# A two-layer decoder trunk: two weight differences placed behind the low parts, and a shorter tail left behind one channel-major matmul

## The chip, the cores and the metric

The kernel runs on one core of one Trainium2 chip. The metric is device time in microseconds of one execution, the median of several runs; lower is better. TensorE (PE, with its weight loads PEld), VectorE (DVE), ScalarE (ACT), GpSimd (POOL) and SyncE (SP, which issues the weight loads from HBM) each work through their own list of instructions in order.

## The reference

256 positions, width 2048, two layers, float32. Cut to what matters:

```python
for l in range(DEPTH):                       # 2
    h = rms_norm(x, norm1_g[l])
    z = h @ w_in[l]                          # 2048 -> 5120
    q, k, v, gu, gv = jnp.split(z, splits, axis=-1)
    attn = dilated_attention(rotary(q), rotary(k), v)          # 8 heads of 128
    gm = chunked_gmlp(gelu(gu), gelu(gv), ...)                 # 8 groups of 128
    x = x + jnp.concatenate([attn, gm], -1) @ w_out[l]
    h2 = rms_norm(x, norm2_g[l])
    x = x + jnp.square(jax.nn.relu(h2 @ w_up[l])) @ w_down[l]  # 2048 -> 8192 -> 2048
return rms_norm(x, final_g)
```

## The kernel before

**Products in two parts.** Every float32 operand is split into a high part (`hi`, a float32r copy made by ScalarE) and a low part (`lo`, the rest, a subtraction on VectorE). A product is three matmuls: high by high, high by low, low by high. Weights come in blocks of 128x1024 (`raw`, 7 buffers), loaded by SP, split on ScalarE (L168, or L186 for half a block) and VectorE (L178, L191), and then used by TensorE. Activations lie in `hs` or `half`, split in the same way (L645 high, L648 low).

**Steps.** All matmul work is a list of steps, one or four weight blocks each, and the program text is written out in the order of that list. `ahead` blocks before a step is due, its high parts are written (`high_to`), then its low parts (`low_to`), then the step's matmuls. Three kinds of step matter. A *natural* step (L464 to L466) has activations as stationary operand. A *channel-major* step (`transposed`, L404) has 128x128 pieces of a weight block as stationary operand, 256 positions as moving one, 24 matmuls per block. A *seven-product* step (`fast`, L434) is used for part of the down matrices: on a 2x2 split of positions and output columns it forms seven products instead of eight, in the manner of Strassen and Winograd, with sums of weights and sums of activations (`shared`). It needs four weight blocks: `Top`, `Bottom` and two `Sums`. There are 76 such steps in the run, each between two channel-major ones; the table `ORDER` and `USUAL` say where.

**The sums of weights.** `Top` and `Bottom` are split for their left halves (`Top`) or whole (`Bottom`). Then `Sums.high` of the first sum forms in place, in the raw buffers, t.left = t.right - t.left (L219) and t.right = b.right - t.right (L220); ScalarE copies that block as the high part of the first sum; VectorE goes on with b.right = b.right - t.left (L223) and b.left = b.right - b.left (L224), from which the second sum's high part is copied. Each of these four runs on 128x512 elements. The low parts of the sums (L178) follow.

**Matmuls left behind.** A seven-product step issues 42 matmuls, of which the last `BEHIND` are not written at the step's end but kept in `left_over`. The next channel-major step writes them after its first `BETWEEN` matmuls. The first of that step's matmuls waits for its high part (from ScalarE), the second for its low part (from VectorE).

Of the kernel before, what the change touches and what calls it, by code (L numbers as in the profile page):

```python
# [32 lines left out]
OP = mybir.AluOpType  # L33
# [32 lines left out]
USUAL = ((7, 9), (2, 3), (13, 14))  # L66
WARM = 11
HALVES = 5
BEHIND, BETWEEN = 3, 2
D_SCORES, D_NORM, D_TURN, D_VALUES = 2, 1, 3, 2  # L70


# [19 lines left out]
def trunk(ctx: ExitStack, tc: tile.TileContext, layout, xT, consts, gains, w, b_sp, w_sp, out):  # L92
# [11 lines left out]
    vec, act, pe = nc.vector, nc.scalar, nc.tensor  # L104
# [40 lines left out]
    class Sub:  # L145
# [4 lines left out]
        def __init__(self, *spec):  # L150
            self.i = len(layout)
            self.kc, self.n = spec[-2:]
            layout.append(spec)
# [7 lines left out]
        def high(self, parts, between=None):  # L161
            self.h = wp.tile([P, 1024], F32R, name="hi", tag="hi", bufs=HI_BUFS)
            self.hi = self.h.rearrange("p (k n) -> p k n", n=self.n)
            m = 1024 // parts
            for j in range(parts):
                if between and j:
                    between()
                act.activation(self.h[:, j * m:(j + 1) * m], self.raw[:, j * m:(j + 1) * m], AF.Copy)  # L168

        def low(self, parts, between=None):  # L170
            lo = wp.tile([P, 1024], F32R, name="lo", tag="lo", bufs=LO_BUFS)
            self.lo = lo.rearrange("p (k n) -> p k n", n=self.n)
            m = 1024 // parts
            for j in range(parts):
                r = slice(j * m, (j + 1) * m)
                if between and j:
                    between()
                vec.tensor_tensor(lo[:, r], self.raw[:, r], self.h[:, r].bitcast(F32), op=OP.subtract)  # L178

    class Top(Sub):  # L180
# [7 lines left out]
        def low(self, parts):  # L188
            lo = wp.tile([P, 1024], F32R, name="lo", tag="lo", bufs=LO_BUFS)
            self.lo = lo[:, 0:512].rearrange("p (k n) -> p k n", k=2)  # L190
            vec.tensor_tensor(self.lo, self.left(), self.hi.bitcast(F32), op=OP.subtract)  # L191

        def left(self):
            return self.raw.rearrange("p (k n) -> p k n", k=2)[:, :, 0:256]
# [6 lines left out]
    class Bottom(Sub):  # L201


        left, right, frees = Top.left, Top.right, 0

    class Sums(Sub):


# [1 line left out]

        def __init__(self, top, bottom, second):
            self.top, self.bottom, self.second = top, bottom, second
            self.n = 512

        def high(self, parts):
            t, b = self.top, self.bottom
            self.raw = (b if self.second else t).raw
            if not self.second:
                vec.tensor_tensor(t.left(), t.right(), t.left(), op=OP.subtract)  # L219
                vec.tensor_tensor(t.right(), b.right(), t.right(), op=OP.subtract)  # L220
            Sub.high(self, 1)
            if not self.second:
                vec.tensor_tensor(b.right(), b.right(), t.left(), op=OP.subtract)  # L223
                vec.tensor_tensor(b.left(), b.right(), b.left(), op=OP.subtract)  # L224
# [287 lines left out]
    def layer(l, n1, n2, n3, last):  # L512
# [130 lines left out]
        def to_half(t, c, src, wait=False):  # L643

            act.activation(t[:, c:c + 2, 0, :], src, AF.Copy)  # L645

            def low():
                vec.tensor_tensor(t[:, c:c + 2, 1, :], src, t[:, c:c + 2, 0, :].bitcast(F32), op=OP.subtract)  # L648

            if wait:  # L650
                behind.append((now[0] + 1, low))
            else:
                low()
# [419 lines left out]
```

## Time and profile before

| what | value |
|---|---|
| median of 3 runs | 2032.55 us (2028.91 to 2033.97) |
| profiled execution | 2032.09 us, span 2030.3 us |
| granted TensorE clock | 0.998 |
| HBM | 394.58 MB read, 205 GB/s over the span |
| L404, matmuls of channel-major steps | 12480 |
| L434, matmuls of seven-product steps | 3192 |

In the rows that follow in the prediction, a timeline row is: start in us from the span's start, duration in us, engine, line, operation, output and inputs by the program's names, shape, and the count of instructions merged into the row; a bracket at its end is idle time of the engine before it and what ended it. A row of the waits is: engine, what it issued, what it waited for, then us in total, times, and the longest. Matmuls are pipelined, so a matmul's duration is longer than the time until the next one starts.

### The profile page before, as it was taken

The numbers are of one execution on the slowest core, as the hardware profiler recorded it, in microseconds if no ns is written. First come the engines' busy times: TensorE is split into PE (matmuls) and PEld (weight loads), VectorE is DVE, ScalarE is ACT, GpSimd is POOL, SyncE is SP. The second block draws the span as 40 slices with busy tenths as digits, with TensorE's granted clock in tenths as the row PEclk, the third lists the DMA queues.
The fourth block names the chain that finished last, engine by engine and source line by source line (L and its number), as shares of the span: only waits on it lengthen the run. The fifth ranks groups of instructions, "written<-read, shape, count | busy, mean of one in ns | idle before, by whom it ended". The sixth has DMA issues, their size and how long they took to land.

```text
span 2030.3 us, 40718 instructions
## 1 busy us (share of the span) xinstructions
PE 2016.9 (99%) x16834; PEld 1979.6 (98%) x16834; DVE 1576.8 (78%) x1950; ACT 1213.2 (60%) x1613; POOL 157.1 (8%) x200
## 2 busy tenths in 40 slices
PE   9999999999999999999999999999999999999997
PEld 7998999999999999999989989999999999999997
DVE  7566766688888898888856667667888898888985
ACT  7565454566566666665545654556666666667654
POOL 0002300000001000100000033000000000010000
PEclk9999999999999999999999999999999999999999
DMA  8554556567677776866664455555676776778562
GB/s 326 192 168 166 187 187 200 175 229 207 217 221 237 244 225 193 243 214 210 204 212 166 167 187 188 188 196 180 217 228 209 226 236 215 239 212 263 183 211 93
DMA packets 126443, 419.27 MB, mean 207 GB/s; under 512 B 14128, under 2 KB 22064, under 8 KB 126256
## 3 DMA queue, kind: packets, MB, share of 16 engines
q1 hardware_dynamic: 110800, 389.86, 56.6%
q0 software_dynamic: 14304, 23.86, 6.8%
q8 instruction: 132, 2.16, 0.4%
q10 hardware_dynamic: 1152, 2.94, 0.4%
q14 instruction: 55, 0.45, 0.1%
HBM read 394.58 MB, written 22.02 MB: 205 GB/s over the span
## 4 chain that ended last, share of the span: by engine, by line
PE 97%; DVE 2%; DMA 1%; ACT 0%; issue 0%; ACTq 0%; SPq 0%; DVEq 0%
PE acc L404 69%; PE acc L434 9%; PE aux L434 8%; PE acc L466 3%; PE acc L465 3%; PE acc L464 3%; DVE lo L178 1%; PE aux L698 0%; PE aux L592 0%; PE aux L634 0%; DMA raw<-in_w 0%; PE aux L621 0%; DVE x L1035 0%; DMA x<-in_xT 0%; PE aux L595 0%
## 5 line engine op out<-in xcount | busy, mean ns | idle before, releaser
L168 ACT ACTIVATE hi<-raw 128x1024 fp32r<-128x1024 f32 (+1 forms) x817 | 836.1, 1051 | 496.2 <-DVE raw L220 232.6
L178 DVE TENSOR_TENSOR lo<-raw,hi 128x1024 fp32r<-128x1024 f32 (+1 forms) x817 | 963.6, 1213 | 155.9 <-ACT hi L168 152.7
L404 PE MATMUL acc<-hs,hi 128*128 128x256 f32 x5632 | 988.1, 277 | 0.0
L404 PEld LDWEIGHTS acc<-hs,hi 128*128 128x128 f32 x5632 | 858.4, 188 | 0.3 <-issue 0.2
L404 PE MATMUL acc<-hs,lo 128*128 128x256 f32 x2816 | 779.0, 277 | 0.0
L404 PEld LDWEIGHTS acc<-hs,lo 128*128 128x128 f32 x2816 | 528.8, 188 | 0.5 <-issue 0.2
L404 PE MATMUL acc<-half,hi 128*128 128x256 f32 x2688 | 462.1, 276 | 0.0
L404 PEld LDWEIGHTS acc<-half,hi 128*128 128x128 f32 x2688 | 406.5, 188 | 0.0
L404 PE MATMUL acc<-half,lo 128*128 128x256 f32 x1344 | 371.1, 276 | 0.0
L404 PEld LDWEIGHTS acc<-half,lo 128*128 128x128 f32 x1344 | 252.4, 188 | 0.0
L871 POOL DMA_DIRECT2D far<-ar x92 | 74.7, 983 | 1158.9 <-ACT ar L874 607.0
L434 PE MATMUL acc<-hi,shared 128*128 128x256 f32 x768 | 139.1, 276 | 0.0
L434 PE MATMUL aux<-hi,half 128*128 128x256 f32 x528 | 120.6, 278 | 0.0
L434 PEld LDWEIGHTS acc<-hi,shared 128*128 128x128 f32 x768 | 119.3, 188 | 0.0
L434 PE MATMUL acc<-lo,shared 128*128 128x256 f32 x384 | 106.5, 277 | 0.6 <-DVE lo L178 0.6
L464 PE MATMUL acc<-hi,hs 128*128 128x512 f32 x256 | 101.3, 396 | 0.2 <-ACT hs L286 0.2
L466 PE MATMUL acc<-hi,hs 128*128 128x512 f32 x256 | 100.8, 394 | 0.0
L465 PE MATMUL acc<-lo,hs 128*128 128x512 f32 x256 | 100.1, 391 | 0.6 <-DVE lo L178 0.6
L648 DVE TENSOR_TENSOR half<-ar,half 128x512 fp32r<-128x512 f32 x72 | 49.7, 690 | 62.3 <-ACT half L645 61.2
L434 PEld LDWEIGHTS aux<-hi,half 128*128 128x128 f32 x528 | 92.9, 188 | 0.0
L434 PE MATMUL aux<-hi,shared 128*128 128x256 f32 x448 | 81.1, 276 | 0.0
L504 DVE TENSOR_TENSOR x<-x,acc 128x512 f32<-128x512 f32 (+1 forms) x49 | 33.0, 674 | 57.7 <-PE acc L404 57.3
(151 smaller groups left out, 1954.0 us busy)
## 6 DMA issues: line engine op xcount, KB each, us to landing
raw<-in_w SPq DMA_DIRECT2D x731, 512.0 KB, 4.6
far<-ar POOLq DMA_DIRECT2D x60, 256.0 KB, 6.3
far<-ar POOLq DMA_DIRECT2D x32, 128.0 KB, 4.4
ar<-far POOLq DMA_DIRECT2D x12, 256.0 KB, 8.9
raw<-in_w SPq DMA_DIRECT2D x10, 256.0 KB, 5.1
x<-in_xT SPq DMA_DIRECT2D x7, 256.0 KB, 5.9
out<-x SPq DMA_DIRECT2D x7, 256.0 KB, 3.0
shared<-in_b_sp ACTq DMA_DIRECT2D x2, 512.0 KB, 8.1
```

The costliest lines, as they stand in the source:

```text
L168: act.activation(self.h[:, j * m:(j + 1) * m], self.raw[:, j * m:(j + 1) * m], AF.Copy)
L178: vec.tensor_tensor(lo[:, r], self.raw[:, r], self.h[:, r].bitcast(F32), op=OP.subtract)
L404: pe.matmul(o, lhsT=lhs, rhs=xs[:, rhs, :], start=(first and j == 0), stop=(last and j == 2), skip_group_check=True)
L434: calls.append(lambda k=k, j=j, lhs=lhs, rhs=rhs: pe.matmul(o[n], lhsT=lhs, rhs=rhs, start=(p == 0 and k == 0 and j == 0 and n in fresh), ...
L464: pe.matmul(ps, lhsT=xh, rhs=hi, start=(k0 + k == 0), stop=False)
L465: pe.matmul(ps, lhsT=xh, rhs=lo, start=False, stop=False)
L466: pe.matmul(ps, lhsT=xl, rhs=hi, start=False, stop=(k0 + k == KC - 1))
L504: vec.tensor_tensor(xj, xj, ps[j][:, 0:S] if alone else pair(ps)[:, j, :], op=OP.add)
L648: vec.tensor_tensor(t[:, c:c + 2, 1, :], src, t[:, c:c + 2, 0, :].bitcast(F32), op=OP.subtract)
L871: nc.gpsimd.dma_start(far[g][:, r], src, **({} if e == max(g, 1) else {"accum_op": OP.add}))
```

## The change

Two parts. First, the two subtractions that form t.left and t.right (L219 and L220 before) leave `Sums.high` and stand right behind the low part of `Top` and of `Bottom` (L192 and L210 after); for that the first `Sums` tells `Bottom` its `Top`. Second, `BEHIND, BETWEEN` go from 3, 2 to 2, 1. The order of ScalarE, GpSimd and SP is not changed.

```diff
--- before.py
+++ after.py
@@ -66,7 +66,7 @@
 USUAL = ((7, 9), (2, 3), (13, 14))
 WARM = 11
 HALVES = 5
-BEHIND, BETWEEN = 3, 2
+BEHIND, BETWEEN = 2, 1
 D_SCORES, D_NORM, D_TURN, D_VALUES = 2, 1, 3, 2
 
 
@@ -189,6 +189,7 @@
             lo = wp.tile([P, 1024], F32R, name="lo", tag="lo", bufs=LO_BUFS)
             self.lo = lo[:, 0:512].rearrange("p (k n) -> p k n", k=2)
             vec.tensor_tensor(self.lo, self.left(), self.hi.bitcast(F32), op=OP.subtract)
+            vec.tensor_tensor(self.left(), self.right(), self.left(), op=OP.subtract)
 
         def left(self):
             return self.raw.rearrange("p (k n) -> p k n", k=2)[:, :, 0:256]
@@ -203,6 +204,11 @@
 
         left, right, frees = Top.left, Top.right, 0
 
+        def low(self, parts):
+            Sub.low(self, 1)
+            t = self.top
+            vec.tensor_tensor(t.right(), self.right(), t.right(), op=OP.subtract)
+
     class Sums(Sub):
 
 
@@ -210,14 +216,12 @@
 
         def __init__(self, top, bottom, second):
             self.top, self.bottom, self.second = top, bottom, second
+            bottom.top = top
             self.n = 512
 
         def high(self, parts):
             t, b = self.top, self.bottom
             self.raw = (b if self.second else t).raw
-            if not self.second:
-                vec.tensor_tensor(t.left(), t.right(), t.left(), op=OP.subtract)
-                vec.tensor_tensor(t.right(), b.right(), t.right(), op=OP.subtract)
             Sub.high(self, 1)
             if not self.second:
                 vec.tensor_tensor(b.right(), b.right(), t.left(), op=OP.subtract)
```

VectorE at the first seven-product step: `lo` with 128x512 is the low part of the top block, the next `lo` that of the bottom block, `raw<-raw` are the four subtractions. Before:

```order
L178 TENSOR_TENSOR lo<-raw,hi 128x1024
L191 TENSOR_TENSOR lo<-raw,hi 128x512
L178 TENSOR_TENSOR lo<-raw,hi 128x1024
L219 TENSOR_TENSOR raw<-raw 128x2x256
L220 TENSOR_TENSOR raw<-raw 128x2x256
L223 TENSOR_TENSOR raw<-raw 128x2x256
L224 TENSOR_TENSOR raw<-raw 128x2x256
```

After:

```order
L178 TENSOR_TENSOR lo<-raw,hi 128x1024
L191 TENSOR_TENSOR lo<-raw,hi 128x512
L192 TENSOR_TENSOR raw<-raw 128x2x256
L178 TENSOR_TENSOR lo<-raw,hi 128x1024
L210 TENSOR_TENSOR raw<-raw 128x2x256
L227 TENSOR_TENSOR raw<-raw 128x2x256
L228 TENSOR_TENSOR raw<-raw 128x2x256
```

One subtraction has moved ahead of the bottom block's low part; the second stands where it stood. At 10 of the 76 steps other work of VectorE lies between the two blocks' low parts, and the first subtraction moves ahead of that too. The first such place, after the change (L652 is L648 of before):

```order
L191 TENSOR_TENSOR lo<-raw,hi 128x512
L192 TENSOR_TENSOR raw<-raw 128x2x256
L652 TENSOR_TENSOR shared<-ar,shared 128x2x256 x2
L178 TENSOR_TENSOR lo<-raw,hi 128x1024
L210 TENSOR_TENSOR raw<-raw 128x2x256
```

TensorE at the end of the second seven-product step. `acc<-hs,...` is the channel-major step, `aux<-...,half` the seventh product. Before:

```order
L434 MATMUL aux<-lo,half 128x256
L434 MATMUL aux<-hi,half 128x256
L404 MATMUL acc_4577<-hs,hi 128x256
L404 MATMUL acc_4577<-hs,lo 128x256
L434 MATMUL aux<-hi,half 128x256
L434 MATMUL aux<-lo,half 128x256
L434 MATMUL aux<-hi,half 128x256
L404 MATMUL acc_4577<-hs,hi 128x256 x2
L404 MATMUL acc_4577<-hs,lo 128x256
```

After:

```order
L438 MATMUL aux<-lo,half 128x256
L438 MATMUL aux<-hi,half 128x256 x2
L408 MATMUL acc_4577<-hs,hi 128x256
L438 MATMUL aux<-lo,half 128x256
L438 MATMUL aux<-hi,half 128x256
L408 MATMUL acc_4577<-hs,lo 128x256
L408 MATMUL acc_4577<-hs,hi 128x256 x2
L408 MATMUL acc_4577<-hs,lo 128x256
```

The channel-major matmul on `lo`, which waits for VectorE, stands three matmuls later; the one on `hi`, which waits for ScalarE, one later.

## The prediction

> **What bounds the kernel now.** I read the page's busy shares first, then the first line of the chain that ended last, then the busy time by stretch, and last what TensorE waits for.
>
> ```profile
> span 2030.3 us, 40718 instructions
> PE 2016.9 (99%) x16834; PEld 1979.6 (98%) x16834; DVE 1576.8 (78%) x1950; ACT 1213.2 (60%) x1613; POOL 157.1 (8%) x200
> ...
> PE 97%; DVE 2%; DMA 1%; ACT 0%; issue 0%; ACTq 0%; SPq 0%; DVEq 0%
> ```
>
> TensorE is busy for 2016.9 of 2030.3 us and carries 97% of the chain. VectorE is at 78% on average, so an edit on VectorE counts only where VectorE is late for TensorE. These two stretches, an ordinary one and one in the up and down matrices near a layer's end, show that there are such places:
>
> ```profile
> 420.00:500.00 80.00, 80.00 (x706) 80.00 (x706) 66.77 (x76) 50.40 (x64) 6.51 (x9) 1.00 0.71 223
> 800.00:811.00 11.00, 10.80 (x94) 10.60 (x93) 10.82 (x12) 5.58 (x7) 0.00 (x0) 1.00 0.61 197
> ```
>
> After the stretch's length the columns are PE, PEld, DVE, ACT and POOL busy, the granted clock, the DMA share and GB/s. In 420 to 500 VectorE has 13 us of 80 free and PE none; in 800 to 811 VectorE is full (10.82 of 11.00) and PE loses 0.20. The clock is 1.00 in both. The lists of what PE and PEld waited for put all of the seven-product line's waits in two rows:
>
> ```profile
> PE acc L434 <- DVE lo L178: 0.6, 3, 0.2
> PEld acc L434 <- DVE lo L178: 1.3, 4, 0.4
> ```
>
> Four waits in the whole run, all for a low part. So the pool from which this change can draw is small, and the rest is the cost of the matmuls' order itself.
>
> **Edit 1, matmuls left behind (3 to 2, after one matmul instead of two).** No matmul is added or taken away; 76 seven-product steps are each followed by a changed row of eight or so. One such place before, on TensorE, with the next 256-column matmuls behind it:
>
> ```profile
> 495.25 0.28 PE L434 MATMUL aux<-hi,half 128*128 128x256 f32 x1
> 495.36 0.28 PE L404 MATMUL acc<-hs,hi 128*128 128x256 f32 x1
> 495.48 0.28 PE L404 MATMUL acc<-hs,lo 128*128 128x256 f32 x1
> 495.60 0.28 PE L434 MATMUL aux<-hi,half 128*128 128x256 f32 x1
> 495.72 0.28 PE L434 MATMUL aux<-lo,half 128*128 128x256 f32 x1
> 495.83 0.28 PE L434 MATMUL aux<-hi,half 128*128 128x256 f32 x1
> 495.95 0.40 PE L404 MATMUL acc<-hs,hi 128*128 128x256 f32 x2
> 496.19 0.28 PE L404 MATMUL acc<-hs,lo 128*128 128x256 f32 x1
> 496.30 0.39 PE L404 MATMUL acc<-hs,hi 128*128 128x256 f32 x2
> ...
> 497.32 0.28 PE L404 MATMUL acc<-hs,hi 128*128 128x256 f32 x1
> ```
>
> Durations overlap, so what a matmul costs is start to start. In the plain row from 496.30 to 497.32 nine matmuls take 1.02 us, 113.3 ns each. In the mixed row from 495.36 to 496.30 eight take 0.94, 117.5 ns each. The mixing costs 0.94 - 8 x 0.1133 = 0.033 us here, and with 76 places 2.5 us in the run. That is all that the order of matmuls costs today. The changed row has the same three switches between the two kinds (434 to 404, back, and to 404 again), but its mixed part is three matmuls long (one and two) and not five (two and three); with the three behind it that still read slow, six instead of eight. I take 6/8 of the cost: -0.6 us. Bounds: all of it goes (-2.5), or it doubles because a lone 404 matmul between two runs of 434 is worse (+2.5, another 0.033 at each of 76). The value lies near the middle, since the nearest row is the same pattern two matmuls longer.
>
> One place shows what the order of waits is worth. Near the end of layer 0 the low part for the next channel-major step was late:
>
> ```profile
> 925.54 0.19 PEld L404 LDWEIGHTS acc<-hs,hi 128*128 128x128 f32 x1
> 925.65 0.28 PE L404 MATMUL acc<-hs,hi 128*128 128x256 f32 x1
> 925.86 0.19 PEld L404 LDWEIGHTS acc<-hs,lo 128*128 128x128 f32 x1
> 925.86 0.39 PE L404 MATMUL acc<-hs,lo 128*128 128x256 f32 x1
> 925.96 0.19 PEld L434 LDWEIGHTS aux<-hi,half 128*128 128x128 f32 x1
> 926.08 0.28 PE L434 MATMUL aux<-hi,half 128*128 128x256 f32 x1
> ```
>
> The matmul on lo starts 0.21 after its forerunner instead of 0.11, and the three left-behind matmuls, which need nothing new, stand behind it: the first starts 0.22 later, because its weights were not loaded while the array waited. Loss: 0.10 + 0.11 = 0.21 us. In the changed order the matmul on lo stands three matmuls (0.34 us) further back, and the one on hi one matmul (0.11 us) further, so both get more time and nothing is asked for sooner; this loss goes: -0.2 us. It is a single place. What stands behind the waiting matmul is then the rest of the channel-major step, which needs the same low part anyway.
>
> The Trainium skill (TensorE: Matmul & The Clock Gate, "Step-by-step: what each phase is for") says that the queue pulls weight loads ahead of running matmuls while matmuls keep their order. By that rule the left-behind weights would be loaded during the wait and this place would give back 0.1 us, not 0.2. The rows at 925.86 and 925.96 speak against it here: the load behind the waiting one did not go ahead.
>
> **Edit 2, two subtractions moved.** 152 of VectorE's instructions move (76 of L219, 76 of L220), none is added. A row at the full stretch:
>
> ```profile
> 802.07 0.68 DVE L191 TENSOR_TENSOR lo<-raw,hi 128x512 fp32r<-128x512 f32 x1
> 802.67 1.22 DVE L178 TENSOR_TENSOR lo<-raw,hi 128x1024 fp32r<-128x1024 f32 x1
> 803.81 0.68 DVE L219 TENSOR_TENSOR raw<-raw 128x512 f32<-128x512 f32 x1
> 804.52 0.69 DVE L220 TENSOR_TENSOR raw<-raw 128x512 f32<-128x512 f32 x1
> 805.25 0.69 DVE L223 TENSOR_TENSOR raw<-raw 128x512 f32<-128x512 f32 x1
> 805.97 0.69 DVE L224 TENSOR_TENSOR raw<-raw 128x512 f32<-128x512 f32 x1
> 806.58 1.22 DVE L178 TENSOR_TENSOR lo<-raw,hi 128x1024 fp32r<-128x1024 f32 x1
> ```
>
> Start to start, a 512-wide one followed by one that does not touch its data takes 0.60 or 0.61 (L191, L224); one followed by an instruction that must wait for it takes 0.71 to 0.73 (L219, L220, L223). The difference, 0.11 us, is the price of two dependent instructions side by side. Before, three such pairs stand here: L219-L220, L220-L223, L223-L224. After, they are the top's lo with the first subtraction (it overwrites what lo has just read), the second subtraction with the third, and the third with the fourth; the second no longer follows the first directly. So three again: 0.72 + 0.60 + 1.14 + 0.72 + 0.72 + 0.61 = 4.51, against 806.58 - 802.07 = 4.51. On VectorE: 0. If I have one pair wrong, it is 0.11 us either way per site.
>
> What moves in time: the bottom's lo ends some 0.7 us later, and the subtraction that ScalarE waits for, with all behind it, ends when it did. ScalarE's wait there is its largest:
>
> ```profile
> ACT hi L168 <- DVE raw L220: 232.6, 76, 5.2
> ```
>
> 3.1 us each time, at every site, and yet PE waits four times only: this wait has cover. It shrinks only where VectorE had stood idle for the bottom's hi. In the full stretch nobody gains, and the late part is the sums' lo, last of the row:
>
> ```profile
> 806.81 0.28 PE L434 MATMUL acc<-lo,shared 128*128 128x256 f32 x1
> ...
> 807.26 0.39 PE L434 MATMUL acc<-hi,shared 128*128 128x256 f32 x2
> 807.85 0.38 PE L434 MATMUL acc<-lo,shared 128*128 128x256 f32 x1 [0.20 <-DVE lo L178]
> ```
>
> At 807.26 two matmuls take 0.59 instead of 0.23: 0.36 lost, and with an unhidden load behind it 0.47; four such waits make at most 1.9 us. They keep their time, since the sum in front of them does: 0, with bounds of -1.9 (all vanish) and +0.5 (0.11 later at each of four). The bottom's lo, now at 804.6 instead of 803.9, is needed at product 2; the row at 806.81 is the second matmul on a low part of product 3, six matmuls before it is 806.1: 1.5 us of cover left. Where that cover was used up, the next thing late would be this lo.
>
> At 10 of 76 sites low parts of the activations' sums stand between the two weights' low parts, and the subtraction goes ahead of them:
>
> ```profile
> 791.40 1.29 DVE L648 TENSOR_TENSOR shared<-ar,shared 128x512 fp32r<-128x512 f32 x2
> ...
> 796.85 1.29 DVE L648 TENSOR_TENSOR shared<-ar,shared 128x512 fp32r<-128x512 f32 x2 [0.25 <-ACT shared L645]
> ```
>
> The pair at 791.40 comes 0.7 us later; the pair at 796.85, which TensorE needs next, has the same work in front of it as before. Cost 0. ScalarE, POOL and SP issue the same in the same order; SP's loads wait for the last reader of raw, which is still the fourth subtraction or the sums' lo.
>
> **Sum.** Against the profiled execution's 2032.09 us (span 2030.3 and 1.8 around it): -0.6 - 0.2 + 0 = 2031.3. The median of the runs is 0.46 above that execution, so 2031.8 as a median.
>
> **Rivals.** (A) The forecast: small change of order, under 1 us. (B) All that can be won is won: the mixing cost 2.5, the late place 0.2 and the four waits 1.9: 2032.55 - 4.6 = 2028.0. For it: the pool exists in the rows. Against: three switches and three dependent pairs remain. Even this is -0.23%. (C) Slower: the lone channel-major matmul is too short a cover for the weights of the two behind it, and one load per site shows, 0.11 us as in the row at 926.08: 76 x 0.11 = 8.4, giving 2041.0. Against: at 495.60 the load behind the second 404 matmul was hidden with the same neighbours. It decides from 0.08 us per site on (6.1 us). By the rule of the Trainium skill above (TensorE: Matmul & The Clock Gate) it could not happen at all, since loads are pulled ahead. (D) The bottom's lo, 0.7 us later, comes too late in the full stretches: say six sites by up to 0.7 us, +4.2 us, 2036.8; against it stand the 1.5 us above. (E) The change doesn't do what it says: VectorE gets back no time because three dependent pairs stay. I hold this true, it is part of A.
>
> **How the numbers follow.** A 0.78, B 0.09, C 0.04, D 0.06, and 0.03 for something not seen (of either sign). 0.3% is 6.1 us, about what a measurement of this kernel can tell from no change; A, B and D lie inside it, C outside. Faster by more 0.03, within 0.91, slower 0.06. The range takes in B and D with half a microsecond beyond each: 2027.5 to 2037.3; the runs shown, 2028.9 to 2034.0, scatter inside it. For A alone it is 2030 to 2034 (bounds of -2.5 and +2.5 on the mixing).
>
> **What the changed profile would show.** PE busy again 99% with the same 16834 matmuls; in the mixed row six start-to-start times of about 117 ns and then 113; at the place near 926 the matmul on lo without its 0.21; VectorE's row per site 4.5 us long with the first subtraction at 0.72 behind the top's lo and the second followed by the third at 0.72; four waits of the seven-product line for lo, as long as now. The prediction is wrong if matmuls behind the lone 404 show 0.2 us start to start at most sites, or if PE's waits for low parts pass some 8 us.

## The result, and the profile after

| | median, us | lowest to highest | runs |
|---|---|---|---|
| before | 2031.82 | 2028.77 to 2033.97 | 21 |
| after | 2034.22 | 2031.79 to 2034.91 | 21 |

The ratio after to before is 1.0012, with a 95% interval of 1.0007 to 1.0018: slower by 0.12%, or 2.4 us, where -0.7 had been forecast. That lies within the 0.3% and within the range, but the sign is wrong and the interval leaves no change out, so there is something to find.

The page of after, its first lines:

```profile
span 2030.1 us, 40718 instructions
PE 2017.2 (99%) x16834; PEld 1980.4 (98%) x16834; DVE 1576.7 (78%) x1950; ACT 1214.1 (60%) x1613; POOL 157.7 (8%) x200
```

And what the seven-product line (L438 now) waited for:

```profile
PEld acc L438 <- DVE lo L178: 1.7, 4, 0.5
PE acc L438 <- DVE lo L178: 0.9, 4, 0.3
```

The matmuls are the same and so is the number of waits; by these rows the four are 0.3 to 0.4 us longer in all than before (0.9 and 1.7 for 0.6 and 1.3), which is far from 2.4. The profiled execution of after took 2031.91 us and is one of its fastest; the profiled one of before took 2032.09. Their spans differ by 0.2 us, so subtracting page from page tells nothing. The loss must be looked for in parts whose size differs from one execution to the next.

It shows in the chain that ended last. A row there is start in us, duration in us, engine, output, line, and how many instructions in unbroken sequence. These rows of before are the same piece of a channel-major step, 94 matmuls between two mixed rows:

```profile
480.43 10.67 PE acc L404 x94
506.35 10.67 PE acc L404 x94
811.06 11.07 PE acc L404 x94
897.77 10.67 PE acc L404 x94
1816.61 10.67 PE acc L404 x94
1901.25 11.07 PE acc L404 x94
```

And of after, where the piece has 95 matmuls because only one matmul stands ahead of the two left behind:

```profile
479.99 10.78 PE acc L408 x95
505.87 10.78 PE acc L408 x95
810.11 10.78 PE acc L408 x95
894.68 11.19 PE acc L408 x95
1814.01 11.20 PE acc L408 x95
1900.78 11.20 PE acc L408 x95
```

10.67 / 94 and 10.78 / 95 are both 113.5 ns for a matmul; 11.07 / 94 and 11.19 / 95 are both 117.8. No row here lies between. TensorE has two rhythms, steady paces, for the same instructions, 4.3 ns apart. No wait stands inside these pieces, and a row of the busy times over a slow piece of before shows the clock granted in full (the columns are those of the prediction's windows):

```profile
811.00:822.00 11.00, 11.00 (x96) 11.00 (x95) 8.85 (x11) 7.78 (x12) 3.51 (x4) 1.00 0.98 269
1816.00:1830.00 14.00, 14.00 (x126) 14.00 (x125) 11.59 (x13) 10.78 (x16) 3.46 (x4) 1.00 0.97 274
```

The second row is, but for its first 0.6 us, a piece in the fast rhythm. Both have a clock of 1.00 and DMA at 0.97 to 0.98, so neither of these makes the difference. The Trainium skill (TensorE: Matmul & The Clock Gate, "Back-to-back issue gap") has one spacing for an isolated matmul of width 256, 262 cycles at 2.4 GHz, by estimate 109 ns; the two rhythms here are both longer, and the measurement decides.

Summed over every matmul's start time, what stands above 113.3 ns in stretches of the slow rhythm is this, in us (0.2 of each sum is two short stretches near 340 and 1345, in every kernel):

| stretch | before | after |
|---|---|---|
| 807 to 876 | 2.55 | fast |
| 892 to 931 | 0.12, ends at 897.7 | 1.43 |
| 1811 to 1875 | 0.13, ends at 1816.6 | 2.41 |
| 1898 to 1937 | 1.43 | 1.47 |
| sum | 4.4 | 5.5 |
| span less the sum | 2025.9 | 2024.6 |

Each stretch begins at one of the four waits for a low part, near 807, 892, 1811 and 1898 us. A pair is the two seven-product steps that work on the same outputs; the waits stand in the second step of the pairs that the table `ORDER` puts at (1, 2), which are called late pairs below. One of the waits in after:

```profile
1810.27 0.39 PE L438 MATMUL acc<-hi,shared 128*128 128x256 f32 x2
1810.92 0.39 PE L438 MATMUL acc<-lo,shared 128*128 128x256 f32 x1 [0.26 <-DVE lo L178]
```

It ends at the next fp32 transposes of a finished group of outputs (L844 of before, L848 of after), or at the second of them. In before it also ended early twice, at the first mixed row behind the wait. After has no such end; one wait of its four, near 807, started nothing.

With that first stretch slow as well, at 2.4 us as in the kernel e1_tail_only below, the profiled 2031.91 would be 2034.3, near the median of 2034.22. The runs fall in two groups: 5 lie from 2031.79 to 2032.68 and 16 from 2034.02 to 2034.91, with nothing between and 2.2 us from middle to middle, about what the first or third stretch costs. Before has no such groups and scatters over 5.2 us. That the groups of after are this stretch on and off is an inference: only one execution of after has a profile.

### The profile page after: what moved, and what is told of

Its sections match the earlier page's. It is cut to its first block, busy times and chain, and to the rows that moved or that the text cites. A ratio compares the mean times of both kernels' runs of the same rounds, so it can differ in the third digit from the quotient of the medians.

```text
span 2030.1 us, 40718 instructions
## 1 busy us (share of the span) xinstructions
PE 2017.2 (99%) x16834; PEld 1980.4 (98%) x16834; DVE 1576.7 (78%) x1950; ACT 1214.1 (60%) x1613; POOL 157.7 (8%) x200
## 4 chain that ended last, share of the span: by engine, by line
PE 96%; DVE 3%; ACT 1%; issue 0%; DVEq 0%; ACTq 0%
PE acc L408 68%; PE acc L438 9%; PE aux L438 8%; PE acc L468 3%; PE acc L470 3%; PE acc L469 3%; DVE lo L178 1%; PE aux L702 0%; PE aux L596 0%; PE aux L638 0%; PE aux L625 0%; PE aux L995 0%; DVE shared L652 0%; DVE x L1039 0%; DVE lo L191 0%
## 5 line engine op out<-in xcount | busy, mean ns | idle before, releaser
L438 PE MATMUL acc<-hi,shared 128*128 128x256 f32 x768 | 139.0, 276 | 0.0
L438 PEld LDWEIGHTS acc<-hi,shared 128*128 128x128 f32 x768 | 119.4, 188 | 0.0
L438 PE MATMUL aux<-hi,half 128*128 128x256 f32 x528 | 111.1, 277 | 0.0
L438 PE MATMUL acc<-lo,shared 128*128 128x256 f32 x384 | 106.5, 277 | 0.9 <-DVE lo L178 0.9
L652 DVE TENSOR_TENSOR half<-ar,half 128x512 fp32r<-128x512 f32 x72 | 49.7, 691 | 62.5 <-ACT half L649 61.4
L438 PEld LDWEIGHTS aux<-hi,half 128*128 128x128 f32 x528 | 87.3, 188 | 0.0
L438 PE MATMUL aux<-hi,shared 128*128 128x256 f32 x448 | 81.3, 277 | 0.0
```

Source lines behind the costliest of these rows:

```text
L438: calls.append(lambda k=k, j=j, lhs=lhs, rhs=rhs: pe.matmul(o[n], lhsT=lhs, rhs=rhs, start=(p == 0 and k == 0 and j == 0 and n in fresh), ...
```

## The experiments

**Theory 1**: an operand that comes late to a seven-product step puts TensorE in the slow rhythm; the mixed row of three behind two sometimes ends it, the row of two behind one never does, so the shorter tail pays for each late operand until the transposes. The rivals: the loss lies in the subtractions on VectorE; the mixed rows or the waits themselves cost more; there is no loss beyond scatter.

### One part of the change alone

```diff
 e1_tail_only: before with
-BEHIND, BETWEEN = 3, 2
+BEHIND, BETWEEN = 2, 1
 e2_subs_only: after with
-BEHIND, BETWEEN = 2, 1
+BEHIND, BETWEEN = 3, 2
```

> The shorter tail alone (2 matmuls left behind, after 1), subtractions as before. Theory 1 (rhythm): after a late low part TensorE goes on at 117.7 ns per matmul instead of 113.3 until the fp32 transposes of a finished group; the row of 3 behind 2 can bring it back to 113.3, the row of 2 behind 1 cannot. Then this kernel has after's time, about 2034 us (+2.4 on before), most runs between 2034 and 2035 and none below 2031.5, and its profile shows slow stretches that reach from a late low part to the next transposes. Theory 2 (VectorE): the moved subtractions make low parts later. Then this kernel has before's time or up to 1.5 us less, 2030.3 to 2031.8.

> The two moved subtractions alone, tail as before (3 behind 2). Theory 1: before's time, 2031.8 within 1 us, with runs scattered over some 4 us from 2029 to 2034, because a slow stretch ends early in some runs and not in others. Theory 2: after's time plus the 1.5 us of mixing that the shorter tail saves, about 2035.5.

Against before on the same chip (2032.16), the tail alone took 2034.25 (2033.87 to 2034.77, 11 runs), 1.0011 [1.0002, 1.002]: nearly all of the 1.0012 that the whole change costs. The subtractions alone took 2033.0 (2030.98 to 2033.83, 11 runs), 1.0004 [0.9995, 1.0013], not to be told from before, with a wide scatter like before's. That interval would still hold a loss like that of the change; that the subtractions cost nothing rests on VectorE's rows further below. The chain of the tail alone has the slow rhythm at all four places:

```profile
479.55 10.78 PE acc L404 x95
809.76 11.20 PE acc L404 x95
896.55 11.19 PE acc L404 x95
1815.88 11.19 PE acc L404 x95
```

Its slow stretches sum to 7.8 us, its span less these is 2024.2. In the subtractions alone the mixed row behind the first wait ended the slow rhythm (0.13 us there), the other three places stayed slow: 5.9, and 2026.2 without. So the tail's rest is 1.7 us shorter than before's (2025.9 to 2024.2; 2026.2 to 2024.6 with the subtractions moved), and the stretches outweigh it. Not all of the 1.7 is the tail's. The chain's first piece of 48 channel-major matmuls starts at 52.31 in before, 52.21 in the subtractions alone, 52.10 in after and 51.67 in the tail alone, ahead of any mixed row: these executions begin up to 0.6 us apart. Less that, the rest is 1.1 to 1.5 us shorter.

### Moving the late operands

```diff
 e4_after_later (on after), e5_before_later (on before)
-ORDER = {1: ((7, 10), (13, 14)), 6: ((11, 14), (1, 2), (6, 7)), 7: ((6, 9), (1, 2)), 8: ()}
+ORDER = {1: ((7, 10), (13, 14)), 6: ((11, 14), (2, 3), (6, 7)), 7: ((6, 9), (2, 3)), 8: ()}
```

> After, with the seven-product steps that stand right behind the start of an up block for e = 6 and 7 placed one channel-major step later (1, 2 becomes 2, 3), so that VectorE has 2.7 us more of TensorE time for the same work. If the four waits for low parts go, theory 1 expects the slow stretches to go too: 5.3 us of slow rhythm in after's profile plus some 2 us of waits, so 2024 to 2027 us for all runs, with a scatter under 1.5 us. Theory 2 expects the waits alone to go, 2 us: 2032.

> Before, with the same later places. Theory 1: no waits and no slow stretches either, and the tail of 3 behind 2 costs the 1.5 us more of mixing that the profiles show in the ordinary stretches: 1.0 to 2.0 us above the after kernel with later places, 2025.5 to 2028.5. Theory 2 expects 2029.8, 2 us below before, and the after kernel with later places above it.

After with the late pairs one place later took 2033.57 (2032.63 to 2033.99), 1.0006 [0.9997, 1.0015]; before with the same 2035.3 (2032.96 to 2037.06), 1.0014 [1.0005, 1.0023]. The late operands did not go, they moved: waits begin at 829.89, 909.65, 1835.69 and 1915.46 of the first, and slow stretches run from there, or from a smaller wait 6 us ahead, mostly to the transposes. Channel-major matmuls now wait for a low part too, twice in each kernel:

```profile
PE acc L408 <- DVE lo L178: 1.3, 2, 0.7
PE acc L404 <- DVE lo L178: 2.2, 2, 1.3
```

The first row is of after with later places, the second of before with them. Both levels missed what theory 1 expected, since its premise, no late operand, was not met. Only the order of the two, the shorter tail ahead by 1.7 us, is as expected, and 0.9 of that lies in these new waits. This pair is inconclusive.

Relieving VectorE instead, by giving to GpSimd the low parts of the activations that stand in front of the late places:

```diff
 e6_after_relief (on after), e7_before_relief (on before)
-        def to_half(t, c, src, wait=False):
+        def to_half(t, c, src, wait=False, eng=vec):
...
-                vec.tensor_tensor(t[:, c:c + 2, 1, :], src, t[:, c:c + 2, 0, :].bitcast(F32), op=OP.subtract)
+                eng.tensor_tensor(t[:, c:c + 2, 1, :], src, t[:, c:c + 2, 0, :].bitcast(F32), op=OP.subtract)
...
-                to_half(hid[e][0], c // P, z, True)
+                to_half(hid[e][0], c // P, z, True, nc.gpsimd if e in (5, 6) and c == 768 else vec)
...
-                to_half(sum_parts[0], k, inner[:, k:k + 2, :])
+                to_half(sum_parts[0], k, inner[:, k:k + 2, :], False, nc.gpsimd if e in (5, 6) and k < 4 else vec)
```

> After, with three low-part subtractions of activations per layer and tight place (e = 5 and 6: the last one of the hidden half, and those of the first two sums) on GpSimd instead of VectorE, some 1.9 us of VectorE's time ahead of the places where the low part of the weights' sum was 0.4 us late. Theory 1 (rhythm): if the low parts are in time, there are no slow stretches: 7.8 us of slow rhythm and 2 us of waits less than the run with the shorter tail alone, so 2024 to 2026.5 us, all runs within 1.5 us. Theory 2 (the time lies in the waits, and the slow stretches come from DMA traffic or chance): 2 us below after, 2032.

> Before, with the same relief of VectorE. Theory 1: no late low parts, no slow stretches, and the longer tail costs its 1.5 us of mixing more: 1.0 to 2.0 us above the after kernel with relief, 2025 to 2028 us. Then the shorter tail is the better one where nothing is late. Theory 2: 2029.8, 2 us below before and 2 us below after with relief.

After with relief took 2038.84 (2038.5 to 2039.05, 5 runs), 1.0036 [1.0022, 1.0049]; before with it 2034.57 (2034.0 to 2037.96, 11 runs), 1.0018 [1.001, 1.0027]. Both were a miss: loads for the seven-product line waited 12 times instead of 4 in the first and 10 times in the second, and slow stretches grew to 9.1 us in the first. The timelines of VectorE and GpSimd in the first show why (rows between are left out):

```profile
787.12 0.69 DVE L805 TENSOR_TENSOR ar<-ar 128x512 f32<-128x512 f32 x1 [1.49 <-POOL half L652]
...
790.63 1.66 DVE L192 TENSOR_TENSOR raw<-raw 128x512 f32<-128x512 f32 x1
...
792.81 1.72 DVE L178 TENSOR_TENSOR lo<-raw,hi 128x1024 fp32r<-128x1024 f32 x1
...
785.79 1.29 POOL L652 TENSOR_TENSOR half<-ar,half 128x512 fp32r<-128x512 f32 x1 [6.23 <-ACT half L649]
...
790.07 3.37 POOL L652 TENSOR_TENSOR shared<-ar,shared 128x512 fp32r<-128x512 f32 x2 [2.16 <-issue]
```

VectorE first stands idle for 1.49 us until GpSimd has written the low part of `half`, a subtraction that takes VectorE itself 0.69 in after. Then, while GpSimd's two subtractions ran, VectorE's 128x512 took 1.66 us instead of 0.69 and its 128x1024 1.72 instead of 1.22; GpSimd's pair took 3.37 against 1.29 for one alone. The two engines hold each other up. The Trainium skill (SBUF — State Buffer, "SBUF: two separate sides") says that a VectorE instruction with two SBUF inputs and a GpSimd one that reads SBUF lock each other out of a shared pair of ports; these rows agree. The two 128x512 of `shared` taken off VectorE here are worth 1.38 us, and it lost 1.47 again in these two rows (0.97 and 0.50).

### A late operand by itself

```diff
 e8_after_late_at_3 (on after), in Sub.low
-                vec.tensor_tensor(lo[:, r], self.raw[:, r], self.h[:, r].bitcast(F32), op=OP.subtract)
+                for _ in range(getattr(self, "times", 1)):
+                    vec.tensor_tensor(lo[:, r], self.raw[:, r], self.h[:, r].bitcast(F32), op=OP.subtract)
 in fast
+            if row0 == 2048 and col0 == 512 and p == 1:
+                upper.times = 3
```

One low part per layer, at an early step with time to spare, is written three times, so that it comes late.

> After, with one low part of a weights' sum written three times (same values) at the second seven-product step of e = 3 in both layers, so that it comes some 0.7 us too late there, at 558 and 1562 us. Theory 1: from there on 117.7 ns per matmul, through all mixed rows, until the first fp32 transposes 310 us later: 2.8 us per 600 matmuls, some 9 us per layer beyond the wait, 18 to 20 us in all if both waits start the slow rhythm, 9 if one does: 2043 to 2056. Theory 2: 1.4 us of waits, 2036.

One run of 2034.20, span 2032.3; expected were 2043 to 2056. The two waits came, 1.0 us each, and behind them the rhythm was fast:

```profile
564.11 10.78 PE acc L409 x95
811.16 10.78 PE acc L409 x95
895.72 11.20 PE acc L409 x95
```

So theory 1 in its strong form, that any late operand starts the slow rhythm, is refuted. At the four places it did so in 30 of 32 cases, over the eight profiled kernels that came to all four in the fast rhythm; the two exceptions are after and this kernel near 807. What sets a start apart from a wait of 1.0 us is open.

### The tail as a switch

```diff
 e3_no_tail (on after)
-                for call in calls[:-BEHIND]:
+                for call in calls:
                     call()
-                left_over.extend(calls[-BEHIND:])
```

> After with no matmuls left behind: a seven-product step ends, and the channel-major step follows with no mixed row. Theory 1 in its strong form: the clean change from activations to weights as stationary operand starts the slow rhythm too, and only a mixed row ends it; then most of the up and down matrices' 11000 matmuls take 4.4 ns more, 35 to 48 us in all: 2065 to 2082. Weak form (only late operands start it): the mixing cost goes, 1.0 to 1.5 us below after: 2032.5 to 2033.

One run of 2040.42, span 2038.7. The strong form there, in which a clean change starts the slow rhythm and only a mixed row ends it, expected 2065 to 2082, the weak one 2032.5 to 2033; both missed. The rhythm changes without any wait, from one step to the next:

```profile
396.90 4.76 PE aux L438 x42
401.66 8.48 PE acc L408 x72
410.14 4.95 PE aux L438 x42
415.09 8.17 PE acc L408 x72
```

4.76 / 42 is 113.3 ns, 8.48 / 72 is 117.8, 4.95 / 42 is 117.9, 8.17 / 72 is 113.5. A clean exit, from seven-product matmuls straight to channel-major ones, turns a fast rhythm slow and a slow one fast. (In the first kind the weights are the moving operand, in the second the stationary one.) By the matmuls' start times, 74 of the 76 exits do so, 38 from fast to slow and 36 from slow to fast; the two that kept the slow rhythm, at 814.6 and 1823.5, stand right behind a late operand. The slow stretches sum to 15.8 us. A mixed row makes that change twice, and so mostly keeps the rhythm it found. This gives the second form of theory 1, theory 3 in the expectations: the change toggles, the mixed row of two behind one toggles twice. (Theory 4 there is that the slow stretches belong to the place, whatever stands there.) The second form foretells two things: a clean exit right behind a late operand ends the slow rhythm; a clean exit at an early step starts one that lasts.

The first, in three kernels:

```diff
 e12_after_clean_late (on after), e14_before_clean_late (on before), e10_tail_only_clean_late (on e1_tail_only)
-                for call in calls[:-BEHIND]:
+                stay = 0 if p == 1 and col0 == 512 and row0 in (5120, 6144) else BEHIND
+                for call in calls[:len(calls) - stay]:
                     call()
-                left_over.extend(calls[-BEHIND:])
+                left_over.extend(calls[len(calls) - stay:])
 e11_after_clean_at_2 (on after): row0 == 1024 instead of row0 in (5120, 6144)
```

The four steps named have no tail; the other 72 keep theirs.

> After, with the same four clean exits. Theory 3: 2034.2 - 7.1 = 2027.1 in runs in which all four late operands leave the slow rhythm; where one leaves the fast one, the clean exit makes it slow and the run is 1.4 or 2.4 us longer, up to 2030. Theory 4: 2034.

> Before (3 left behind 2), with the same four clean exits. Theory 3: the mixing of the longer tail costs some 1.5 us more than in the kernel with the shorter tail and clean exits: 2027.5 to 2030, below before by 2 to 4. Theory 4: before's 2031.7.

> The shorter tail alone (subtractions as before), but with no tail at the four steps where the low part is late (second seven-product step of the late pair, e = 6 and 7, both layers). Theory 3 (toggle): TensorE has two rhythms, 113.3 and 117.7 ns; a late operand leaves it in the slow one nearly always, each change from a seven-product to a channel-major matmul toggles it, so a row with a tail has two toggles and keeps what it found, and a step without a tail has one. Then the clean exit behind the late operand ends the slow rhythm there: 7.6 us of slow stretches less 0.5 up to the exit, 2034.25 - 7.1 = 2027.1, between 2026 and 2028.5 in all runs. Theory 4 (the slow stretches belong to the place: DMA traffic or a full VectorE): 2034 as without the edit.

Against before on the same chip (2031.15, 27 runs), after with clean exits took 2029.25 (2027.0 to 2030.75, 11 runs), 0.9986 [0.9977, 0.9994]: faster than both kernels. Its profiled execution, the fastest of the 11, has the slow rhythm end at the clean exit at all four places; here a piece has 96, since no matmul stands ahead of a tail:

```profile
809.91 10.89 PE acc L408 x96
894.47 10.90 PE acc L408 x96
```

Its slow stretches sum to 0.6 us, and the span of 2025.2 less these is 2024.6, the same as for after: nothing else has changed by as much. Before with the same exits took 2030.64 (2028.9 to 2032.78), 0.9998 [0.9989, 1.0006]; all four exits ended the rhythm, and its profiled span is 2027.1 with 1.1 slow, 2026.0 without. Of these 1.1, 0.4 lie in two short stretches further on, near 923 and 1927, each behind a channel-major matmul on `lo` that came 0.1 us late, as at 925.86 of before; after has neither. The tail alone with them took 2031.32 (2027.31 to 2032.92), 0.9998 [0.9989, 1.0007]; in its profile three of four exits ended the rhythm and the one near 892 did not:

```profile
810.14 10.90 PE acc L404 x96
894.72 11.31 PE acc L404 x96
```

So the exit ends it in 11 of 12 profiled cases, not always. The medians won less than that suggests: for the tail alone with clean exits 2026 to 2028.5 had been expected in all runs, and 2 of 11 lie there; for before with them 2027.5 to 2030, and 4 of 11 lie there. The profiled executions are among the fastest of their kernels, and in the slower ones more exits may have failed, which no profile shows.

The second:

> After, with one clean exit per layer at an ordinary step in time: the second seven-product step of the late pair of e = 2, at 475 and 1480 us. Theory 3: the exit toggles the fast rhythm to slow, and the mixed rows keep it so up to the late pair of e = 6, some 2930 matmuls by 4.35 ns = 12.7 us per layer, 25 in all: 2055 to 2061. Theory 4, and a reading in which the switch costs only its own few matmuls: 2034.

One run of 2058.56, span 2056.8, in the range expected of theory 3. Two exits, no late operand near them, and the slow rhythm stands from 480 to 881 and from 1498 to 1900, over 56 mixed rows that all keep it:

```profile
480.02 11.31 PE acc L408 x96
507.01 11.20 PE acc L408 x95
```

Without its slow stretches (34.2 us) the span would be 2022.6, 2 us less than for after. About 1 us of that is the mixed rows, counted in that sum though the fast rhythm pays 0.018 us for each as well; another 1.1 is two of the four waits, near 807 and 1811 in after, which did not occur here.

## Why the prediction was right or wrong

**The mixing cost: right sign, too small.** The mixed row of after, on TensorE, in the fast rhythm:

```profile
495.13 0.28 PE L408 MATMUL acc<-hs,hi 128*128 128x256 f32 x1
495.25 0.28 PE L438 MATMUL aux<-lo,half 128*128 128x256 f32 x1
495.37 0.28 PE L438 MATMUL aux<-hi,half 128*128 128x256 f32 x1
495.48 0.28 PE L408 MATMUL acc<-hs,lo 128*128 128x256 f32 x1
495.60 0.39 PE L408 MATMUL acc<-hs,hi 128*128 128x256 f32 x2
495.83 0.28 PE L408 MATMUL acc<-hs,lo 128*128 128x256 f32 x1
495.94 0.39 PE L408 MATMUL acc<-hs,hi 128*128 128x256 f32 x2
```

Six matmuls take 0.70 here, 116.7 ns each. In the chain, from one such piece to the next, lie the same matmuls and two sites: 480.43 to 506.35 is 25.92 us before, 479.99 to 505.87 is 25.88 after. That is 0.02 a site and 1.5 us for 76, where 0.6 had been forecast. By the start times of 47 such rows in each, a mixed row stands 0.039 us above the plain pace before and 0.018 after: half of the cost is left, not six eighths. The spans less slow stretches agree: 1.1 to 1.5 lower with the shorter tail when the different beginnings are taken off, the late place below included. In the slow rhythm the saving is not there: behind the first late place, where before and the tail alone are both slow, the changed row is some 0.015 longer. Rival C, an unhidden load at each site, has no such row.

**The late place near 926: right, 0.2.** In after the matmul on lo follows its forerunner at the pace around it:

```profile
924.08 0.28 PE L438 MATMUL aux<-hi,half 128*128 128x256 f32 x1
924.20 0.28 PE L408 MATMUL acc<-hs,lo 128*128 128x256 f32 x1
```

**VectorE's edit: right, 0.** The row at the full stretch, of after:

```profile
801.32 0.68 DVE L191 TENSOR_TENSOR lo<-raw,hi 128x512 fp32r<-128x512 f32 x1
802.04 0.69 DVE L192 TENSOR_TENSOR raw<-raw 128x512 f32<-128x512 f32 x1
802.65 1.22 DVE L178 TENSOR_TENSOR lo<-raw,hi 128x1024 fp32r<-128x1024 f32 x1
...
805.84 1.22 DVE L178 TENSOR_TENSOR lo<-raw,hi 128x1024 fp32r<-128x1024 f32 x1
```

801.32 to 805.84 is 4.52, where 4.51 was forecast: rival E's mechanism held. The bottom's low part, 0.7 us later (1.33 behind the start of the top's instead of 0.60), made no new wait, so rival D did not happen.

**The four waits: the step that failed.** They kept their number, as forecast, and were priced at their length: 0.47 us each, "They keep their time", a change of 0. The length itself was nearly right: by start times the four lost 1.66 us before and 2.01 after. What follows a wait was taken to be unaffected. In fact the 1.4 to 2.4 us of slow rhythm that run on behind most of them are the larger part of their cost, and how long they last hangs on the mixed row that the change alters. The sentence "That is all that the order of matmuls costs today" is the same error seen from the other side: a mixed row was priced by its own eight matmuls, and it also decides the pace of the hundreds behind it. The row at 811.06 in the chain, 11.07 us for 94 matmuls beside 10.67 for the same 94 at 480.43, stood in the trace of before and was not used.

Put together: -1.5 for the mixing, -0.2 for the late place, +0.3 for the waits, and four slow stretches of 7.6 us (the tail alone) in place of the 4.2 of before's profile give +2.0 against that execution, +2.3 against before's median, which lies 0.3 below it; +2.4 was measured. These terms overlap by some tenths, since rows inside a slow stretch are counted in it. Laid matmul beside matmul from 52 us on, the tail alone ends 2.1 us behind before's profile. The points named as signs in the changed profile came out as written or nearly so, and the sign of the result was still wrong: they all tested the terms of the sum, and none what the sum had left out. Rivals B, C and D did not happen either; what did belongs to the 0.03 that was kept for something not seen.

**What stays open.** Why the change of kind toggles the rhythm inside TensorE, and why not always; which of the things that change there (the role of the weights, the output tile, the activations' tile) does it, since no kernel changes one alone; why a late operand starts the slow rhythm at the four places and a longer wait at an early step did not; why the row of three behind two, as the first mixed row behind a late operand, ends it in 3 of 8 cases (before and the subtractions alone) and the row of two behind one in none of 7 (after and the tail alone). A version with no late operand was not obtained, so the cost of after without them is known only as span less stretches. Which stretches were slow in the executions without a profile, and so how the medians come about, is inferred.

## What to carry to other kernels

Divide duration by count for equal pieces of the chain along the whole run: where a busy engine runs the same instructions at two paces, a wait or a change of order may cost far more behind its place than in it. Price an edit on such an engine by what it does to the pace that follows, and test that with a kernel in which only the switch differs. Where an execution may or may not fall into the slow pace, compare spans less the slow stretches, and the groups in the runs' times, not one profile with another.

## What the hardware showed that was not expected

TensorE held two steady rhythms, 113.5 and 117.8 ns for each load and matmul of width 256, at a granted clock of 1.00 and for up to 400 us on end. A change from matmuls with moving weights to matmuls with stationary ones switched between them at 74 of 76 places, with no wait needed. And GpSimd subtractions beside VectorE's own stretched one of the latter from 0.69 to 1.66 us, and one of GpSimd's kept VectorE waiting for 1.49; after with that relief stood at 1.0036 of before and without it at 1.0012.
